# Attention probabilities transposed by DMA for six of eight head pairs, and seven half products in place of eight for gate and up of two of six feed-forward chunks

## The chip, the core and the metric

The kernel runs on one core of a Trainium2 chip. Five engines work side by side: TensorE (PE in the profile; its weight loads are PEld), VectorE (DVE), ScalarE (ACT), GpSimd (POOL) and SyncE (SP), which here only issues DMAs. The metric is the time of one execution on the device in microseconds; lower is better.

## The reference

Two layers of a streaming encoder on x of 256 tokens by 1024, all in float32. Cut to what matters:

```python
def swiglu_ffn(h, w_up, w_down):                   # w_up: 1024 x 5632, w_down: 2816 x 1024
    gate, up = jnp.split(h @ w_up, 2, axis=-1)
    return (jax.nn.silu(gate) * up) @ w_down

for l in range(2):
    x = x + 0.5 * swiglu_ffn(rms_norm(x, g_ffn1[l]), w_up1[l], w_down1[l])
    h = rms_norm(x, g_mix[l]); z = h @ w_in[l]     # LRU x and gate | q | k | v | forget logits | branch gates
    y_lru = (gelu(z_lg) * rg_lru(conv(z_lx), ...)) @ w_lru_out[l]
    # 16 heads of 64, per block of 128 queries:
    #   s = qn @ kn.T * scale + cum_q - cum_k, causal;  p = softmax(s);  o = p @ v
    y_attn = o @ w_attn_out[l]
    x = x + (gate_lru * y_lru + gate_attn * y_attn) @ w_o[l]
    x = x + 0.5 * swiglu_ffn(rms_norm(x, g_ffn2[l]), w_up2[l], w_down2[l])
```

## The kernel before

Every large product is made of three matmuls in a rounded float32 format: each operand is split into a high part and the rest, and high x high, high x low and low x high add up in one PSUM bank (`visit`, L397 to L399). Weights pass through in tiles of 256 rows by 512 columns, 128x1024 on chip, 512 KB each, numbered in one list `hcs` in the order of use. `emit_dma` (L307) loads the next tile into one of RAW = 5 buffers `raw`, on SP's queue. `emit_hi` (L331) casts it on ACT to `whi`, `emit_lo` (L340) subtracts on DVE, raw minus high, into `wlo`; RING = 6 of each exist, and a cast can go ahead once the tile six places earlier has had its last matmul. When `emit_lo` has read a raw buffer, the load of the next tile is issued into it. `block` runs a piece of 1024 x 512 weights: four tiles, first for token block 0 and then for token block 1, twelve matmuls of 512 columns a tile.

The feed-forward (`ffn`) walks over the 2816 hidden columns in six chunks `CH`, five of 512 and one of 256. For a chunk it runs gate (`ev_g`: SiLU on ACT, L637), up (`ev_u`: times the gate on DVE, L642) and then `down` of the chunk before it: for either half of the output two tiles and two token blocks. Gate and up end in PSUM banks `z`, `down` in `x` and `y`. The chunk's hidden values are turned by `h_chain`: `turn` copies them as 16-bit halves into a temporary tile (L315 on DVE or L318 on ACT, whichever the planner holds to be free first), SP issues a DMA transpose (L517), and a second copy puts the halves back; `split_seg` (L502 on ACT, L504 on DVE) makes the high and low parts.

In the mixing stage (`mix`) attention runs as chains beside the projections. `pair_chain(j)` handles two heads: eight score matmuls (L1008), a masked minimum on DVE (L1024), exponentials on ACT (L1033), scaling, six 128x128 transposes on PE (`quad`, L481), two copies out of PSUM into `pt` (L315, L318), and `pv_chain` multiplies with the values (L1070). At most NLIVE = 2 pairs are under way. After the gates and the LRU output projection the kernel needs all pairs (`S.need(att)`) before the attention output projection.

The order on every engine is fixed when the program is built. A planner (`Sched`) keeps an estimated time for each engine; after each half tile of matmuls its `hook` steps the chains that are due. The hardware then runs each engine's instructions in that order, each waiting for its semaphores. GpSimd has little work: powers for the norms (L551, L950), constants at the start, and DMAs of small rows. The large scratch tiles are NSLOT = 12 slots of 8 KB a partition, handed out by `slot` and given back by `free`.

## Time and profile before

| | us |
|---|---|
| median of three runs | 1269.91 (1269.89 to 1270.96) |
| the profiled execution | 1269.92 |
| its span, first to last instruction | 1268.2 |
| PE busy | 1257.6 (99%) |
| DVE busy | 825.4 (65%) |
| ACT busy | 804.8 (63%) |
| POOL busy | 69.5 (5%) |
| mean granted TensorE clock | 1.000 of full speed |

Feed-forwards lie at about 12 to 190, 455 to 640, 640 to 818 and 1082 to 1268 us, mixing between them. Times in rows are microseconds from the start of the span unless ns is said; a matmul's shown length includes its pipeline, so that lengths of neighbours overlap. `x3` is a count. What stands in brackets after an instruction is the idle time of its engine before it and who ended that.

### The profile page before, as it was taken

Reading aid. Unit: us, or ns where it says so; the run is one execution under the profiler, and the core shown is the slowest. Engines: PE = TensorE matmul, PEld = TensorE weight load, DVE = VectorE, ACT = ScalarE, POOL = GpSimd, SP = SyncE. Lnnn points to the kernel's source line nnn. Section 1 sums busy time; section 2 is a strip of 40 time slices with the busy share of each in tenths; the row PEclk is TensorE's granted clock in tenths of the full one; section 3 lists DMA queues with packets and bytes.
Section 4 is the critical chain, followed back from the end, with each engine's and each line's share of the span. In section 5 each row is a group of like instructions: output and inputs, shape, how many; then the busy total and the mean of one; then the engine's idle time right before and its main releaser. Section 6 shows DMA issues by size and latency. Waiting matters only on the chain.

```text
span 1268.2 us, 16349 instructions
## 1 busy us (share of the span) xinstructions
PE 1257.6 (99%) x5961; PEld 1039.6 (82%) x5961; DVE 825.4 (65%) x1164; ACT 804.8 (63%) x1076; POOL 69.5 (5%) x89
## 2 busy tenths in 40 slices
PE   9999999999999999999999999999999999999998
PEld 7888888888777888888888888888887878888887
DVE  6655558798676666555575545678977767655553
ACT  6657557886767556555566555679757764665553
POOL 4000000002200000000000000000042000000000
PEclk9999999999999999999999999999999999999999
DMA  7967769676444568676678777597764345687762
GB/s 258 264 207 225 217 172 277 161 218 202 148 141 150 168 198 217 209 208 207 179 220 217 213 216 216 158 249 190 210 206 149 126 150 182 193 222 216 216 199 76
DMA packets 193489, 248.80 MB, mean 196 GB/s; under 512 B 73672, under 2 KB 86144, under 8 KB 193408
## 3 DMA queue, kind: packets, MB, share of 16 engines
q1 hardware_dynamic: 191472, 244.49, 64.8%
q0 software_dynamic: 1920, 3.26, 1.0%
q8 instruction: 47, 0.77, 0.2%
q14 instruction: 34, 0.28, 0.1%
q10 hardware_dynamic: 16, 0.00, 0.0%
HBM read 229.88 MB, written 2.10 MB: 183 GB/s over the span
## 4 chain that ended last, share of the span: by engine, by line
PE 94%; DVE 3%; ACT 1%; DMA 1%; issue 1%; SPq 0%; POOL 0%; ACTq 0%; DVEq 0%
PE x L397 14%; PE x L399 13%; PE x L398 13%; PE z L398 12%; PE z L397 12%; PE z L399 12%; PE y L397 4%; PE y L399 4%; PE y L398 4%; PE z L481 2%; PE z L1008 1%; PE z L818 1%; DVE wlo L340 1%; PE y L1070 1%; DMA raw<-in_w_up_dram 1%
## 5 line engine op out<-in xcount | busy, mean ns | idle before, releaser
L340 DVE TENSOR_TENSOR wlo<-raw,whi 128x1024 fp32r<-128x1024 f32 x423 | 510.3, 1221 | 218.8 <-ACT whi L331 211.4
L331 ACT CAST whi<-raw 128x1024 fp32r<-128x1024 f32 x423 | 440.3, 1049 | 209.2 <-PE z L399 118.0
L397 PE MATMUL x<-whi,s 128*128 128x512 f32 x800 | 322.4, 403 | 4.8 <-DVE nat L954 2.8
L399 PE MATMUL x<-whi,s 128*128 128x512 f32 x800 | 312.5, 391 | 0.0
L398 PE MATMUL x<-wlo,s 128*128 128x512 f32 x800 | 312.2, 390 | 0.0
L398 PE MATMUL z<-wlo,s 128*128 128x512 f32 (+1 forms) x752 | 279.5, 372 | 0.1
L397 PE MATMUL z<-whi,s 128*128 128x512 f32 (+1 forms) x752 | 279.3, 371 | 0.0
L399 PE MATMUL z<-whi,s 128*128 128x512 f32 (+1 forms) x752 | 279.1, 371 | 0.0
L397 PEld LDWEIGHTS x<-whi,s 128*128 128x128 f32 x800 | 150.3, 188 | 38.8 <-issue 2.9
L399 PEld LDWEIGHTS x<-whi,s 128*128 128x128 f32 x800 | 150.2, 188 | 33.3 <-DVE s L504 0.9
L398 PEld LDWEIGHTS x<-wlo,s 128*128 128x128 f32 x800 | 150.5, 188 | 29.4 <-DVE wlo L340 0.6
L398 PEld LDWEIGHTS z<-wlo,s 128*128 128x128 f32 x752 | 141.7, 188 | 25.9 <-DVE wlo L340 1.8
L397 PEld LDWEIGHTS z<-whi,s 128*128 128x128 f32 x752 | 141.7, 188 | 24.4
L399 PEld LDWEIGHTS z<-whi,s 128*128 128x128 f32 x752 | 141.7, 188 | 24.4
L318 ACT COPY tmp<-nat 128x1024 uint16<-128x1024 uint16 (+1 forms) x88 | 96.3, 1114 | 76.2 <-DMA nat<-tmp 68.2
L397 PE MATMUL y<-whi,s 128*128 128x512 f32 x208 | 82.3, 396 | 0.0
L399 PE MATMUL y<-whi,s 128*128 128x512 f32 x208 | 81.1, 390 | 0.0
L398 PE MATMUL y<-wlo,s 128*128 128x512 f32 x208 | 81.0, 390 | 0.0
L642 DVE SCALAR_TENSOR_TENSOR nat<-z,rstd,nat 128x512 f32<-128x512 f32 (+1 forms) x48 | 33.9, 706 | 57.9 <-PE z L399 57.9
L504 DVE TENSOR_TENSOR s<-tmp,s 128x512 fp32r<-128x512 f32 (+1 forms) x71 | 46.6, 657 | 27.4 <-ACT s L502 26.9
L637 ACT ACTIVATE nat<-z,rstd 128x512 f32<-128x512 f32 (+1 forms) x46 | 30.0, 652 | 47.1 <-PE z L399 47.0
L502 ACT CAST s<-tmp 128x512 fp32r<-128x512 f32 (+1 forms) x71 | 42.0, 592 | 20.6 <-DVE tmp L531 19.8
(161 smaller groups left out, 891.0 us busy)
## 6 DMA issues: line engine op xcount, KB each, us to landing
raw<-in_w_up_dram SPq DMA_DIRECT2D x175, 512.0 KB, 4.6
raw<-in_w_in_dram SPq DMA_DIRECT2D x112, 512.0 KB, 4.4
raw<-in_w_down_dram SPq DMA_DIRECT2D x88, 512.0 KB, 4.4
raw<-in_w_lru_out_dram SPq DMA_DIRECT2D x16, 512.0 KB, 3.8
raw<-in_w_attn_out_dram SPq DMA_DIRECT2D x16, 512.0 KB, 3.8
raw<-in_w_o_dram SPq DMA_DIRECT2D x16, 512.0 KB, 4.3
s<-ones_d POOLq DMA_DIRECT2D x16, 128.0 KB, 4.4
tmp<-in_b_gate_dram SPq DMA_DIRECT2D x8, 256.0 KB, 4.3
```

What stands on the lines that cost most here:

```text
L318: nc.scalar.copy(out_, in_)
L331: nc.scalar.copy(hi, raws[i])
L340: nc.vector.tensor_tensor(out=lo, in0=raws.pop(i), in1=f32(hi), op=ALU.subtract)
L397: nc.tensor.matmul(acc, lhsT=lhs(0, k0 + kk)[:, ts], rhs=hi[:, kk, :], start=st, stop=False)
L398: nc.tensor.matmul(acc, lhsT=lhs(0, k0 + kk)[:, ts], rhs=lo[:, kk, :], start=False, stop=False)
L399: nc.tensor.matmul(acc, lhsT=lhs(1, k0 + kk)[:, ts], rhs=hi[:, kk, :], start=False, stop=sp)
L481: nc.tensor.transpose(dst_ps[:, j * P:(j + 1) * P], src[:, j * P:(j + 1) * P], ident)
L502: nc.scalar.copy(hi, t)
L504: nc.vector.tensor_tensor(out=lo, in0=t, in1=f32(hi), op=ALU.subtract)
L637: nc.scalar.activation(s[tok][0], acc, AF.Silu, scale=rs(tok))
L642: nc.vector.scalar_tensor_tensor(out=h, in0=acc, scalar=rs(tok), in1=h, op0=ALU.mult, op1=ALU.mult)
L818: nc.tensor.matmul(ps[:, g, :], lhsT=wax[0][:, g, n, :], rhs=xr[0][:, n, :], start=True, stop=True)
```

## The change

Gate and up of chunks 2 and 4 (`SEVEN`) are one product of a 2 x 2 block matrix (token block by half of k) with another (half of k by gate or up). In place of eight block products seven are made, of sums of blocks (Winograd's form): 84 matmuls of 512 columns instead of 96. The four weight blocks "11", "12", "22", "21" (half of k; gate, up) are loaded by eight DMAs straight into five slots, all at the moment when the load ahead of them is issued. GpSimd makes four sums of weight blocks, t3 = 22 - 12, t1 = 12 - 11, t2 = t3 + 11, t4 = 21 - t2, each in two operations on 128x1024. The products run in the order 11, t1, t2, 21, t3, 22, t4, each over two tiles that are cast and subtracted as before but used for one product only. Once a feed-forward, GpSimd also makes sums of the normalised input, in six operations, which are split once. The results are put together by seven additions on DVE (each with one operand in PSUM) and one copy on ACT, then go through SiLU and product as before.

In attention, pairs 0 to 5 of eight transpose their probabilities with `turn`: a copy to 16-bit halves, a DMA transpose of 128x768 words, and a copy back, in place of six PE transposes and two copies. Four pairs may be under way instead of two; six `pair` buffers take the place of `pr` and `pt`.

To make room RAW goes from 5 to 4; the constants `ones`, `lft` and `g1row` move to pooled tiles (`lft` is now filled by two DVE memsets in every layer), the buffers of `logsig` go from two to one; and the transposes of the small parameter rows come 45 us earlier in the plan. The diff, cut to its core:

```diff
-RAW = 5
+RAW = 4
 NSLOT = 12
 NNAT = 4
 NTMP = 3
-NLIVE = 2
+NLIVE = 4
+NPAIR = 6
 LEAD = 3
 SLACK = 2.5
 IDLE = 1.6
 HSTEP = 3.0
+GPS = 2.3
...
+SEVEN = (2, 4)
...
-        hcs.append((w[r0:r0 + nk * P, c0:c0 + ncol].rearrange("(k p) n -> p k n", p=P), nk, ncol))
+        loads.append((w[r0:r0 + nk * P, c0:c0 + ncol].rearrange("(k p) n -> p k n", p=P), len(hcs)))
+        hcs.append((nk, ncol))
+        uses.append(NT)
+    ORDER = ("11", "t1", "t2", "21", "t3", "22", "t4")
+    class Seven:
+        def __init__(self):
+            self.i0 = len(hcs)
+            self.t, self.chain = {}, None
+        def index(self, name, u):
+            return self.i0 + 2 * ORDER.index(name) + u
+        def part(self, name, u):
+            return self.t[name][0][:, 2 * u:2 * u + 2]
+        def load(self, name, u, src):
+            if not self.t:
+                for k in ("11", "12", "22", "21", "t3"):
+                    self.t[k] = slot([P, 4, 512])
+            nc.sync.dma_start(out=self.part(name, u), in_=src)
+            if name != "12":
+                raws[self.index(name, u)] = self.part(name, u), 0.0
+            if (name, u) == ("21", 1):
+                self.chain = S.add(self.sums(), S.now + 6.0, "g")
+        def sums(self):
+            def op(name, u, dst, a, b, f):
+                o = self.part(dst, u)
+                nc.gpsimd.tensor_tensor(out=o, in0=self.part(a, u), in1=self.part(b, u), op=f)
+                raws[self.index(name, u)] = o, S.use("g", GPS)
+            for u in range(2):
+                op("t3", u, "t3", "22", "12", ALU.subtract)
+                yield S.t["g"], "g"
+                op("t1", u, "12", "12", "11", ALU.subtract)
+                yield S.t["g"], "g"
+            for name, dst, a, b, f in (("t2", "11", "t3", "11", ALU.add), ("t4", "21", "21", "11", ALU.subtract)):
+                for u in range(2):
+                    while nxt["lo"] <= self.index(dst, u):
+                        yield S.now + 0.5, "g"
+                    op(name, u, dst, a, b, f)
+                    yield S.t["g"], "g"
+        def release(self):
+            for t in self.t.values():
+                free(t)
+    sevens = []
+    def plan_seven(w, f0):
+        st = Seven()
+        sevens.append(st)
+        for name, r0, c0 in (("11", 0, f0), ("12", 0, FF + f0), ("22", 512, FF + f0), ("21", 512, f0)):
+            for u in range(2):
+                r = r0 + 256 * u
+                loads.append((w[r:r + 256, c0:c0 + 512].rearrange("(k p) n -> p k n", p=P), (st, name, u)))
+        for _ in range(14):
+            hcs.append((2, 512))
+            uses.append(1)
...
+            if c in SEVEN:
+                plan_seven(wu, f0)
+            else:
+                plan_block(wu, f0, n)
+                plan_block(wu, FF + f0, n)
...
-        src, nk, ncol = hcs[i]
+        src, i = loads.pop(0)
+        nk, ncol = hcs[i]
         t = new(raw_p, [P, nk, ncol], "raw")
         for c in range(cuts):
             ks = slice(c * nk // cuts, (c + 1) * nk // cuts)
             nc.sync.dma_start(out=t[:, ks], in_=src[:, ks])
-        raws[i] = t
+        raws[i] = t, 0.0
+        while loads and isinstance(loads[0][1], tuple):
+            src, (st, name, u) = loads.pop(0)
+            st.load(name, u, src)
...
-        emit_dma()
+        if uses[i] == NT:
+            emit_dma()
...
+        def sums_chain():
+            for tok in range(NT):
+                for hf in range(2):
+                    yield nrm.done[tok, hf]
+            xh, xl = nrm.xT[0][0], nrm.xT[1][0]
+            a, b = slot([P, KD, T]), slot([P, 4, 4, P])
+            for q in range(2):
+                yield S.t["g"], "g"
+                ks = slice(4 * q, 4 * q + 4)
+                nc.gpsimd.tensor_tensor(out=a[0][:, ks], in0=f32(xh[:, ks]), in1=f32(xl[:, ks]), op=ALU.add)
+                S.use("g", GPS)
+            A = lambda tok, q: a[0][:, 4 * q:4 * q + 4, tok * P:(tok + 1) * P]
+            B = lambda i: b[0][:, i]
+            for i, u, v, f in ((0, A(1, 0), A(1, 1), ALU.add), (1, B(0), A(0, 0), ALU.subtract),
+                               (2, A(0, 0), A(1, 0), ALU.subtract), (3, A(0, 1), B(1), ALU.subtract)):
+                yield S.t["g"], "g"
+                nc.gpsimd.tensor_tensor(out=B(i), in0=u, in1=v, op=f)
+                S.use("g", GPS / 2)
+            free(a)
+            sums[0], sums[1] = slot([P, 4, 4, P], F32R), slot([P, 4, 4, P], F32R)
+            yield S.t["g"], "a"
+            for q in range(2):
+                ii = slice(2 * q, 2 * q + 2)
+                yield from split_seg(b[0][:, ii], sums[0][0][:, ii], sums[1][0][:, ii], 1024)
+                yield S.now, "a"
+            free(b)
...
+        def seven(c):
+            st = sevens.pop(0)
+            S.need(sums_c)
+            xh = lambda tok, q: lambda e, k: nrm.xT[e][0][:, 4 * q + k, tok * P:(tok + 1) * P]
+            xs = lambda i: lambda e, k: sums[e][0][:, i, k, :]
+            w = slot([P, 4, 512])
+            s1, u2, u4, c22 = (w[0][:, i] for i in range(4))
+            h, b5 = {}, []
+            def prod(name, lhs_, fin):
+                b, r = zbank()
+                for u in range(2):
+                    visit(st.index(name, u), b, lhs_, 2 * u, None, u == 0, u == 1, (lambda: fin(b, r)) if u else None)
...
+            def after_1(b, r):
+                nc.scalar.copy(s1, b)
+                S.use("a", act_c(512))
+                r.free = True
+            def after_6(b, r):
+                plus(u2, b, s1)
+                r.free = True
+                plus(u4, b5[0], u2)
+            def after_2(b, r):
+                end = plus(s1, b, s1)
+                r.free = True
+                gate(0, s1, end)
+            def after_7(b, r):
+                plus(u2, b, u2)
+                r.free = True
+                plus(c22, b5[0], u2)
+                b5[1].free = True
+            def after_3(b, r):
+                end = plus(u4, b, u4)
+                r.free = True
+                up(0, u4, end)
+            def after_4(b, r):
+                end = plus(u2, b, u2)
+                r.free = True
+                up(1, c22, gate(1, u2, end))
+            prod("11", xh(0, 0), after_1)
+            prod("t1", xs(0), lambda b, r: b5.extend((b, r)))
+            prod("t2", xs(1), after_6)
+            prod("21", xh(0, 1), after_2)
+            prod("t3", xs(2), after_7)
+            prod("22", xs(3), after_3)
+            prod("t4", xh(1, 1), after_4)
...
+                assert hpos[0] == sevens[0].i0
+                seven(c)
+            else:
+                block(lhs, ev_g, xbank if c < mixed else zbank, n, nrm if c == 0 else None, c < mixed)
+                block(lhs, ev_u, zbank, n)
...
+            lft, rl = new_tmp([P, NT + 1, P])
+            nc.vector.memset(lft[:, :NT], 0.0)
+            nc.vector.memset(lft[:, NT], 1.0)
...
-            pr = new(att_p, [P, 2, 3 * P], "pr")
-            mn = new(sm_p, [P, 4], "mn")
-            sums = new(sm_p, [P, 4], "sums")
+            pr, rp = new_pair()
...
-            yield end, "p"
-            pz = []
-            for e in range(2):
-                pz.append(zbank())
-                quad(pr[:, e], pz[e][0], 3)
-            if j >= 2:
-                yield pv_c[j - 2]
-            pt = new(att_p, [P, 2, 3 * P], "pt")
-            end = 0.0
-            for e in range(2):
-                yield S.now, "a"
-                end = max(end, copy_any(pt[:, e], pz[e][0][:, :3 * P], 3 * P, S.now))
-                pz[e][1].free = True
-            pv_c[j] = S.add(pv_chain(j, pt), end, "p", True, LATE)
-        def pv_chain(j, pt):
+            if j < H // 2 - 2:
+                yield end, "a"
+                pt, rt = new_pair()
+                b6 = lambda t: t.rearrange("p e (m t) -> p (e m) t", t=P)
+                yield from turn(pr.rearrange("p e n -> p (e n)"), rp, b6(pt), b6(pt), end)
+                end = S.cur.ready
+            else:
+                yield end, "p"
+                pz = []
+                for e in range(2):
+                    pz.append(zbank())
+                    quad(pr[:, e], pz[e][0], 3)
+                rp.free = True
+                pt, rt = new_pair()
+                for e in range(2):
+                    yield S.now, "a"
+                    end = max(end, copy_any(pt[:, e], pz[e][0][:, :3 * P], 3 * P, S.now))
+                    pz[e][1].free = True
+            pv_c[j] = rt.user = S.add(pv_chain(j, pt, rt), end, "p", True, LATE)
+        def new_pair():
+            r = S.claim(att_ring, NPAIR)
+            return new(att_p, [P, 2, 3 * P], "pair"), r
+        def pv_chain(j, pt, rt):
...
-                live.append(S.add(pair_chain(j), S.now, "p", True, LATE))
+                pairs.append(S.add(pair_chain(j), S.now, "p", True, LATE))
+                live.append(pairs[j])
...
-        yield S.now + 70.0, "p"
+        yield S.now + 25.0, "p"
...
```

## Rows read from the trace of the kernel before

**Rows 1.** The page: busy time of engines, and shares of the ending chain.
```profile
PE 1257.6 (99%) x5961; PEld 1039.6 (82%) x5961; DVE 825.4 (65%) x1164; ACT 804.8 (63%) x1076; POOL 69.5 (5%) x89
...
PE 94%; DVE 3%; ACT 1%; DMA 1%; issue 1%; SPq 0%; POOL 0%; ACTq 0%; DVEq 0%
```

**Rows 2.** Busy time by stretch: a `down` piece, then gate and up of chunk 2.
```profile
core 0: us, PE busy (x) PEld busy (x) DVE busy (x) ACT busy (x) POOL busy (x), PEclk, DMA share, GB/s
...
500.00:511.00 11.00, 11.00 (x50) 9.12 (x49) 5.98 (x6) 6.76 (x8) 0.00 (x0) 1.00 0.95 268
511.00:533.00 22.00, 22.00 (x98) 18.21 (x97) 11.77 (x12) 11.46 (x14) 0.00 (x0) 1.00 0.56 179
```

**Rows 3.** Timeline of PE: start, length; first matmuls of chunk 2 and behind it.
```profile
511.03 0.39 PE L397 MATMUL z<-whi,s 128*128 128x512 f32 x1
...
532.79 0.39 PE L397 MATMUL x<-whi,s 128*128 128x512 f32 x1
```

**Rows 4.** Instructions by line and shape: count | busy us, mean ns | idle before.
```profile
L340 DVE TENSOR_TENSOR wlo<-raw,whi 128x1024 fp32r<-128x1024 f32 x423 | 510.3, 1221 | 218.8 <-ACT whi L331 211.4
L331 ACT CAST whi<-raw 128x1024 fp32r<-128x1024 f32 x423 | 440.3, 1049 | 209.2 <-PE z L399 118.0 <-PE x L399 53.7 <-ACT tmp L318 12.9
...
L318 ACT COPY tmp<-nat 128x1024 uint16<-128x1024 uint16 x72 | 85.2, 1207 | 56.5 <-DMA nat<-tmp 56.5
...
L504 DVE TENSOR_TENSOR s<-tmp,s 128x512 fp32r<-128x512 f32 x63 | 43.2, 686 | 20.1 <-ACT s L502 19.7
...
L315 DVE COPY tmp<-nat 128x1024 uint16<-128x1024 uint16 x24 | 16.7, 698 | 3.6 <-DMA nat<-tmp 3.0
...
L318 ACT COPY pt<-z 128x384 f32<-128x384 f32 x20 | 8.8, 480 | 11.7 <-PE z L481 11.6
```

**Rows 5.** Timeline of POOL at the start: start, length.
```profile
0.80 0.20 POOL masks.py:197 MEMSET ident<- 128x128 f32 x1 [0.29 <-POOLq L1285]
1.08 0.29 POOL masks.py:199 TENSOR_SCALAR_AFFINE_SELECT ident<-ident 128x128 f32<-128x128 f32 x1
...
1.83 0.31 POOL L1190 MEMSET posm<- 128x256 f32 x1
```

**Rows 6.** Timeline of POOL: four power operations.
```profile
189.73 0.56 POOL L551 TENSOR_TENSOR rstd<-msum,mhalf 128x1 f32<-128x1 f32 x1 [80.72 <-DVE msum L549]
...
298.81 1.67 POOL L950 TENSOR_TENSOR rq<-rq,mhalf 128x8 f32<-128x8 f32 x1 [57.72 <-DVE rq L948]
...
311.91 2.57 POOL L950 TENSOR_TENSOR rq<-rq,mhalf 128x8 f32<-128x8 f32 x1 [3.46 <-DVE rq L948]
...
461.43 0.87 POOL L551 TENSOR_TENSOR rstd<-msum,mhalf 128x1 f32<-128x1 f32 x1 [5.80 <-DVE msum L549]
```

**Rows 7.** Timeline of DVE beside those four.
```profile
189.47 0.68 DVE L588 SCALAR_TENSOR_TENSOR xn<-y,xn 128x512 f32<-128x512 f32 x1
...
299.60 1.22 DVE L340 TENSOR_TENSOR wlo<-raw,whi 128x1024 fp32r<-128x1024 f32 x1 [0.87 <-ACT whi L331]
...
311.73 3.69 DVE L340 TENSOR_TENSOR wlo<-raw,whi 128x1024 fp32r<-128x1024 f32 x3
...
461.20 0.68 DVE L504 TENSOR_TENSOR s<-tmp,s 128x512 fp32r<-128x512 f32 x1
```

**Rows 8.** Timeline of DVE ahead of chunk 2 of the second feed-forward.
```profile
486.47 2.59 DVE L340 TENSOR_TENSOR wlo<-raw,whi 128x1024 fp32r<-128x1024 f32 x2 [0.52 <-ACT whi L331]
...
501.02 2.35 DVE L340 TENSOR_TENSOR wlo<-raw,whi 128x1024 fp32r<-128x1024 f32 x2
```

**Rows 9.** The page, DMA issues: count, size, median us to landing.
```profile
raw<-in_w_up_dram SPq DMA_DIRECT2D x175, 512.0 KB, 4.6
...
nat<-tmp SPq DMA_TRANSPOSE x64, 4.6
```

**Rows 10.** Line L340 alone: count, ns min/median/max, first and last start.
```profile
L340 DVE TENSOR_TENSOR wlo<-raw,whi x423: 1198/1224/1228, 10.0 to 1249.3; 128x1024 fp32r<-128x1024 f32 x141
```

**Rows 11.** Busy time by stretch, as in rows 2: the attention pairs of layer 0.
```profile
330.00:395.00 65.00, 63.91 (x350) 50.57 (x349) 46.91 (x129) 49.59 (x116) 6.65 (x3) 1.00 0.40 131
```

**Rows 12.** The ending chain in order of time: start, us, what; one pair's transposes.
```profile
366.19 0.65 PE z L481 x6
```

## The prediction: what the rows say the change will do

> **What bounds the kernel now.** I read the page first: TensorE (PE) is busy for 99% of the span, and 94% of the chain that ended last is PE [rows 1]. Then the timeline of PE inside one gate-and-up chunk: first matmul of the chunk at 511.03 us, first matmul of the next piece at 532.79, so 96 matmuls in 21.76 us, 0.2267 us from start to start with no gap [rows 3]. The 0.39 us that a single one shows is its pipelined length, not its price. The granted clock is 1.00 throughout, so a matmul taken away is worth 0.2267 us as long as the rest keeps up. The rest is VectorE (DVE) and ScalarE (ACT), which split every weight tile (ACT casts `whi`, DVE subtracts to get `wlo`): in that chunk DVE works 11.77 of 22 us, ACT 11.46, and GpSimd (POOL) not at all [rows 2]. So there is room, but it has to be filled exactly where the change needs it.
>
> **What leaves PE.** A chunk of gate and up has 2 token blocks x 2 outputs x 8 k x 3 terms = 96 matmuls. Seven products of 4 k x 3 terms are 84. Twelve fewer, times 0.2267, is 2.72 us a chunk; two chunks in each of four feed-forwards make eight, so 21.8 us. The six transposes of a pair take 0.65 us on PE [rows 12]; six pairs in two layers are 12 x 0.65 = 7.8 us. Together 29.6 us is the most the change can give: 1269.9 - 29.6 = 1240.
>
> **What comes on DVE and ACT for one such chunk.** The seven products use 14 tiles of 128x1024, each for one product, where the ordinary chunk uses 8 tiles for two tokens each. So 14 casts and 14 subtractions instead of 8: six more of 1.05 us on ACT and six more of 1.22 us on DVE (1.13 back to back: two ended 2.35 us after the first began) [rows 4, 8]. Seven additions from PSUM on DVE, at the 0.69 us of a 128x512 operation [rows 4], are 4.8 us, and one 128x512 copy on ACT. PE needs a new tile every 6 x 0.2267 = 1.36 us; alone, DVE at 1.13 plus 0.34 for the additions' share is a little over that, and ACT at 1.05 is under it. The six ring buffers can carry it over such a deficit, if they are full at the start.
>
> **The window that decides.** I lay the new chunk where chunk 2 of the second feed-forward lies now. The eight direct loads are issued together, behind the last load of the `down` piece before them, which waits for a raw buffer: with four raw buffers that is the subtraction that ended at 486.47 + 2.59 = 489.06 [rows 8]. A 512 KB load lands 4.4 to 4.6 us after issue [rows 9], and at the 268 GB/s of the busy `down` stretch [rows 2] each further one takes 1.96 us. The fifth of the eight (block "22", first half), which the first POOL operation needs, is the sixth in line: 489.1 + 4.5 + 5 x 1.96 = 503.4. PE wants the last of the 14 tiles at 511.03 + 13 x 1.36 = 528.7. So 25.3 us, in which all eight POOL operations and twelve of the 14 subtractions (two, on block "11", need no sum and now stand at 501.02) must be through.
> - DVE in it: 12 x 1.13 + two `L504` splits of the previous chunk and the gate-times-up, 3 x 0.69, = 15.7 us with both inputs in SBUF; six additions with a PSUM input, 4.1 us. Sum 19.8 of 25.3: it fits alone.
> - ACT: 12 x 1.05, two SiLU, one copy, two casts, at most two copies of 1.2: about 18 of 25.3. It fits.
> - POOL: no row shows a POOL operation on two tiles of 1024 elements a partition. The nearest: a memset of 128 elements 0.20 us, of 256 elements 0.31, so 0.86 ns an element and 0.09 fixed; an affine select, which also reads, 0.29 at 128 elements, so a read adds 0.70 ns an element [rows 5]. Two reads and a write: 0.09 + 1.024 x (0.86 + 1.40) = 2.4 us. Bounds: four memsets of 256, 1.24 us, and three times that, 3.7. I take 2.4: 19.2 us for eight. It fits alone.
>
> **DVE against POOL.** Now the rows that make me doubt it. POOL's power operation on 128x8 took 1.67 us at 298.81, and 2.57 at 311.91, where a DVE subtraction of two SBUF tiles had begun 0.18 us earlier and had about 1.05 to go. On 128x1 it took 0.87 us beside the two-input `L504` (461.20), but 0.56 beside `L588` (189.47), one of whose inputs is PSUM [rows 6, 7]. So a POOL operation that reads SBUF waits for the end of a DVE operation with two SBUF inputs, and not for one with a PSUM input. The other direction is not shown: POOL's reads here are of 8 elements and over at once (the subtraction at 299.60 began inside a POOL operation and took its normal 1.22 [rows 6, 7]). If POOL's reads hold DVE in the same way, the times add: 15.7 + 19.2 = 34.9 us into 25.3, 9.6 us late. If only the read part holds (2 x 0.70 x 1.024 = 1.43 us an operation, 11.4 in all): 15.7 + 11.4 = 27.1, 1.8 us late. I take 6 us, near the middle.
> The Trainium skill (SBUF — State Buffer, section "Who interferes with whom") states this as a rule: a DVE operation with two SBUF inputs and a GpSimd operation that reads SBUF exclude each other, and whichever comes second waits for the whole of the first. The trace agrees with it for POOL coming second (2.57 against 1.67 us) and shows nothing for DVE coming second. By the rule the whole-operation end, 9.6 us late, would hold. A price of its own has GPSIMD Engine Reference, section "Performance versus the Vector engine" of the Trainium skill: 4497 ns for 2048 elements, so an estimate of 2.25 us here, by which the chunk would be 8.4 us late; no run here shows it.
>
> **The other parts.** Each feed-forward also makes sums of the normalised input: six POOL operations (two of full size, four of half: 9.6 us), two casts, two subtractions, in chunks 0 and 1, whose pieces load DVE much as those of [rows 2] do; taken at 1 us a feed-forward, bounds 0 and 3, 4 us in all. A pair's two copies of 128x1536 uint16 cost at most 1.5 x 1.21 on ACT or 1.5 x 0.70 on DVE each, in place of two of 0.48 [rows 4]: 2.7 us more on ACT or about 1.1 on DVE a pair. Between 330 and 395 us ACT works 49.6 of 65 and DVE 46.9 [rows 11]; six pairs shared between them fit. The transpose's landing (4.6 us [rows 9]) lengthens a pair, but four live pairs take the place of two. I give 1 us back a layer, bounds 0 and 4: -7.8 + 2 = -6. The transposes of h, issued on SP behind the eight loads, land up to 8 us later; the ACT copy that waits for them holds the casts behind it, but `down` needs them only after the chunk: 0 now, up to 2 us a chunk if casts of the sums stand behind it. At nothing: one raw buffer fewer (four loads ahead at 2.72 us of PE each still exceed 4.6 us of landing; without that cover a load's rest, 1 to 2 us a tile), the constants moved to pooled tiles, the earlier row transposes, memsets moved to DVE (under 1 us a layer, beside matmuls).
>
> **The sum.** Forecast: 8 x (6.0 - 2.72) = +26, sums +4, attention -6: +24 us. The profiled execution took 1269.92 us, its span 1268.2 and 1.7 around it, and the median is 1269.91, so no correction: **1294 us**. With the two ends of the lock, 1.8 and 9.6 us late: 8 x (-0.9) - 6 + 4 = -9, 1261; and 8 x 6.9 + 4 - 6 = +53, 1323.
>
> **Rivals.**
> - *POOL does not hold DVE (faster).* Then only POOL's own row counts: six operations (sums t3, t1, t2) from 503.4 at 2.4 us end at 517.8, cast and subtraction make it 520, and PE wants that tile at 511.03 + 5 x 1.36 = 517.8: some 1 to 2 us late a chunk, less if loads land faster. 8 x (1.2 - 2.72) - 6 = -18: **1252**, from 1242 (never late, 1 us kept on the rest) to 1260. For it: no subtraction of the 423 was ever stretched (1198 to 1228 ns is their whole spread [rows 10]). Against it: none ever came second to a long POOL read. It decides as soon as a subtraction that starts inside a POOL operation ends in 1.22 us.
> - *The two cancel.* Lock on the reads only, or POOL earlier than I place it: late by 2 to 3.5 us a chunk, 1262 to 1276, middle **1269**.
> - That the 84 matmuls don't appear can't be: the counts are fixed in the code.
>
> **How the numbers follow.** Forecast case (1276 to 1323) 0.50; POOL harmless (1242 to 1262) 0.40; cancelling 0.10. A measurement here tells 0.2%, about 2.5 us. Of the cancelling case 0.06 lie within that, 0.03 below, 0.01 above: faster 0.43, same 0.06, slower 0.51. Cases of both signs hold the chance; the likeliest one's own range is 1276 to 1316. The range for 8 in 10 leaves out about a tenth on each side: 1246 to 1316.
>
> **What the profile after would show.** Right: `wlo` subtractions of 2 to 3.5 us in chunks 2 and 4, beside POOL operations; POOL operations over 3 us; PE waiting for `wlo` there by 4 us or more a chunk; the other chunks as before. The rival: subtractions still at 1.22, POOL at about 2.4 throughout, a chunk of gate and up within 20 to 21 us. The attention step is right if the transposes of `pr` fall from 96 to 24 and the stretch between its ends is some 3 us a layer shorter. I am wrong on the loads if the first POOL operation of a chunk starts far from 7 to 8 us ahead of the chunk's first matmul (503.4 against 511.0), and wrong altogether if the gap comes from SP's queue or from DMA waits of ACT.

## The result, and the profile after

The changed kernel takes **1380.38 us** (1378.45 to 1384.25) against 1269.91 before: ratio 1.0868, 95% interval 1.0855 to 1.0880. Slower was the forecast, but at 1294 us, with a range that ended at 1316: the forecast was 86 us short.

The page of the changed kernel, to be held against [rows 1]: busy time, the granted TensorE clock in 40 slices, and the ending chain.

```profile
PE 1268.7 (92%) x5793; PEld 1021.6 (74%) x5793; DVE 1013.1 (74%) x1266; ACT 880.7 (64%) x1154; POOL 308.5 (22%) x176
...
PEclk9879999999999999999999999999999999999999
...
PE 58%; DVE 17%; DMA 11%; issue 7%; ACT 4%; POOL 2%; SPq 0%; DVEq 0%; ACTq 0%; POOLq 0%
DVE wlo L414 12%; PE x L478 11%; PE x L479 10%; PE x L480 10%; DMA nat<-tmp 6%; PE z L479 5%; PE z L478 5%; PE z L480 5%; DVE s L582 2%; DMA raw<-in_w_up_dram 2%; PE y L478 2%; PE y L480 2%; PE y L479 2%; DMA raw<-in_w_down_dram 2%; DVE s L755 1%
```

TensorE has 168 matmuls and transposes fewer (96 and 72, as counted), and yet is busy 11 us longer; the chain has left it for DVE and DMA. The instructions by line and shape (count, busy us, mean ns, idle before), to be held against [rows 4]; `L414` is the old `L340`, `L582` the old `L504`, `L280` the sums of weights on POOL, `L755` the seven additions:

```profile
L414 DVE TENSOR_TENSOR wlo<-raw,whi 128x1024 fp32r<-128x1024 f32 x359 | 453.3, 1286 | 92.8 <-ACT whi L405 89.6 <-PE z L480 0.3
...
L414 DVE TENSOR_TENSOR wlo<-s,whi 128x1024 fp32r<-128x1024 f32 x112 | 185.6, 1697 | 64.2 <-ACT whi L405 64.2
L280 POOL TENSOR_TENSOR s<-s,s 128x1024 f32<-128x1024 f32 x64 | 183.9, 2894 | 341.0 <-DMA s<-in_w_up_dram 292.7 <-DVE wlo L414 47.0
...
L582 DVE TENSOR_TENSOR s<-tmp,s 128x512 fp32r<-128x512 f32 x63 | 60.1, 955 | 33.2 <-ACT s L580 32.9
L755 DVE TENSOR_TENSOR s<-z,s 128x512 f32<-128x512 f32 x56 | 38.3, 684 | 0.6
```

Subtractions for the seven products take 1697 ns in the mean in place of 1221 (half of them at most 1216, the longest 3443), splits 955 in place of 686; the additions, one of whose inputs is PSUM, are not stretched (684).

Where the time went is read by stage. Each stage ends with the second of two `rstd` operations on POOL (before: 200.70, 461.43, 645.64, 827.90, 1088.57 us), here three of the changed kernel in the timeline of POOL:

```profile
249.78 0.86 POOL L629 TENSOR_TENSOR rstd<-msum,mhalf 128x1 f32<-128x1 f32 x1 [12.79 <-DVE msum L627]
...
505.77 0.87 POOL L629 TENSOR_TENSOR rstd<-msum,mhalf 128x1 f32<-128x1 f32 x1 [5.79 <-DVE msum L627]
...
716.62 0.56 POOL L629 TENSOR_TENSOR rstd<-msum,mhalf 128x1 f32<-128x1 f32 x1 [12.53 <-DVE msum L627]
```

Differences of such starts, for this kernel and for runs told below (us; ff is a feed-forward, the last one to the end of the span):

| | ff 1 | mixing | ff 2 | ff 3 | mixing | ff 4 |
|---|---|---|---|---|---|---|
| before | 200.7 | 260.7 | 184.2 | 182.3 | 260.7 | 179.6 |
| after | 249.8 | 256.0 | 210.9 | 204.3 | 256.2 | 199.6 |
| attention part alone (e1) | 203.7 | 259.2 | 187.4 | 184.2 | 256.1 | 179.8 |
| POOL additions in the kernel before (e6) | 210.1 | 261.3 | 195.2 | 194.4 | 260.7 | 190.4 |
| no weight sums (e2) | 231.8 | 255.8 | 191.9 | 194.1 | 256.0 | 184.9 |
| the same, rows early, loads spread (e9) | 218.9 | 255.9 | 188.8 | 188.7 | 256.3 | 177.4 |
| no sums, no additions (e14) | 209.2 | 256.4 | 180.7 | 178.9 | 255.8 | 174.1 |

The mixing stages gain 4.5 us each; the feed-forwards lose 49, 27, 22 and 20.

How such a loss comes about shows in chunk 2 of the second feed-forward, where the prediction laid its window. The timeline of SP's queue, ACT, POOL, DVE and PE there, line by line in that order of engines:

```profile
535.14 6.43 SPq L271 DMA_DIRECT2D s<-in_w_up_dram  x8
...
544.51 5.57 SPq L595 DMA_TRANSPOSE nat<-tmp  x1
...
554.57 1.36 ACT L392 COPY tmp<-nat 128x1024 uint16<-128x1024 uint16 x1 [7.88 <-DMA nat<-tmp]
...
547.21 16.16 POOL L280 TENSOR_TENSOR s<-s,s 128x1024 f32<-128x1024 f32 x6 [26.90 <-DMA s<-in_w_up_dram]
...
556.86 1.50 DVE L414 TENSOR_TENSOR wlo<-s,whi 128x1024 fp32r<-128x1024 f32 x1 [9.15 <-ACT whi L405]
558.29 2.88 DVE L582 TENSOR_TENSOR s<-tmp,s 128x512 fp32r<-128x512 f32 x1
561.09 4.50 DVE L414 TENSOR_TENSOR wlo<-s,whi 128x1024 fp32r<-128x1024 f32 x2
...
559.71 0.39 PE L478 MATMUL z<-whi,s 128*128 128x512 f32 x1
564.51 0.51 PE L479 MATMUL z<-wlo,s 128*128 128x512 f32 x1 [4.42 <-DVE wlo L414]
...
566.37 0.63 PE L478 MATMUL z<-whi,s 128*128 128x512 f32 x1
566.80 0.63 PE L479 MATMUL z<-wlo,s 128*128 128x512 f32 x1
```

The transpose of h, issued behind the eight direct loads, lands at 554.54, 10 us after its issue; ACT waits 7.88 us with the copy of it, the casts stand behind that copy, and DVE has nothing to subtract for 9.15 us. POOL meanwhile adds, mostly alone. When the casts come, POOL is still at it: a split of 0.69 us takes 2.88, two subtractions 4.50, and PE stops for 4.42 us. The stretches (us, busy us of PE, PEld, DVE, ACT, POOL, then the granted clock, DMA share, GB/s):

```profile
550.00:555.00 5.00, 5.00 (x24) 4.14 (x23) 0.00 (x0) 0.43 (x1) 4.87 (x3) 1.00 1.12 346
...
560.00:565.00 5.00, 0.58 (x3) 0.44 (x3) 5.00 (x3) 3.16 (x4) 3.37 (x2) 1.00 0.00 0
565.00:570.00 5.00, 5.00 (x17) 3.92 (x16) 5.00 (x6) 4.78 (x6) 1.40 (x1) 0.66 0.02 3
```

DVE works 0 of 5 us in the first stretch, and 5 of 5 in the other two; behind PE's gap of 4.42 us the granted clock is 0.66, and matmuls start 0.43 us apart instead of 0.227 (the levels of 1.2 and 2.4 GHz). On the page, a transpose of h lands 5.9 us after issue in the median, 4.6 before [rows 9], and a direct load after 9.2:

```profile
s<-in_w_up_dram SPq DMA_DIRECT2D x64, 512.0 KB, 9.2
...
nat<-tmp SPq DMA_TRANSPOSE x64, 5.9
```

### The profile page after: what moved, and what is told of

It reads as the page before. It is cut to its first block, busy times and chain, and to the rows that moved or that the text cites. A ratio compares the mean times of both kernels' runs of the same rounds, so it can differ in the third digit from the quotient of the medians.

```text
span 1376.7 us, 16385 instructions
## 1 busy us (share of the span) xinstructions
PE 1268.7 (92%) x5793; PEld 1021.6 (74%) x5793; DVE 1013.1 (74%) x1266; ACT 880.7 (64%) x1154; POOL 308.5 (22%) x176
## 4 chain that ended last, share of the span: by engine, by line
PE 58%; DVE 17%; DMA 11%; issue 7%; ACT 4%; POOL 2%; SPq 0%; DVEq 0%; ACTq 0%; POOLq 0%
DVE wlo L414 12%; PE x L478 11%; PE x L479 10%; PE x L480 10%; DMA nat<-tmp 6%; PE z L479 5%; PE z L478 5%; PE z L480 5%; DVE s L582 2%; DMA raw<-in_w_up_dram 2%; PE y L478 2%; PE y L480 2%; PE y L479 2%; DMA raw<-in_w_down_dram 2%; DVE s L755 1%
## 5 line engine op out<-in xcount | busy, mean ns | idle before, releaser
L414 DVE TENSOR_TENSOR wlo<-raw,whi 128x1024 fp32r<-128x1024 f32 x359 | 453.3, 1286 | 92.8 <-ACT whi L405 89.6
L405 ACT CAST whi<-raw 128x1024 fp32r<-128x1024 f32 x359 | 368.3, 1047 | 165.1 <-PE x L480 44.9
L479 PE MATMUL x<-wlo,s 128*128 128x512 f32 x800 | 316.1, 395 | 13.7 <-DVE wlo L414 13.7
L478 PE MATMUL z<-whi,s 128*128 128x512 f32 (+1 forms) x720 | 273.4, 380 | 10.3 <-ACT whi L405 9.5
L480 PE MATMUL z<-whi,s 128*128 128x512 f32 (+1 forms) x720 | 272.1, 378 | 0.0
L280 POOL TENSOR_TENSOR s<-s,s 128x1024 f32<-128x1024 f32 x64 | 183.9, 2894 | 341.0 <-DMA s<-in_w_up_dram 292.7
L414 DVE TENSOR_TENSOR wlo<-s,whi 128x1024 fp32r<-128x1024 f32 x112 | 185.6, 1697 | 64.2 <-ACT whi L405 64.2
L392 ACT COPY tmp<-nat 128x1024 uint16<-128x1024 uint16 (+1 forms) x92 | 100.6, 1095 | 81.9 <-DMA nat<-tmp 79.7
L405 ACT CAST whi<-s 128x1024 fp32r<-128x1024 f32 x112 | 114.2, 1047 | 34.4 <-POOL s L280 24.4
L629 POOL TENSOR_TENSOR rstd<-msum,mhalf 128x1 f32<-128x1 f32 x12 | 8.2, 684 | 414.2 <-DVE msum L627 414.2
L582 DVE TENSOR_TENSOR s<-tmp,s 128x512 fp32r<-128x512 f32 (+1 forms) x71 | 63.5, 895 | 47.4 <-ACT s L580 47.0
L1145 POOL TENSOR_TENSOR rq<-rq,mhalf 128x8 f32<-128x8 f32 x16 | 34.9, 2182 | 249.7 <-DVE rq L1143 236.4
L478 PE MATMUL y<-whi,s 128*128 128x512 f32 x208 | 82.7, 397 | 0.0
```

The costliest lines, as they stand in the source:

```text
L280: nc.gpsimd.tensor_tensor(out=o, in0=self.part(a, u), in1=self.part(b, u), op=f)
L392: nc.scalar.copy(out_, in_)
L405: nc.scalar.copy(hi, raws[i][0])
L414: nc.vector.tensor_tensor(out=lo, in0=raws.pop(i)[0], in1=f32(hi), op=ALU.subtract)
L478: nc.tensor.matmul(acc, lhsT=lhs(0, k0 + kk)[:, ts], rhs=hi[:, kk, :], start=st, stop=False)
L479: nc.tensor.matmul(acc, lhsT=lhs(0, k0 + kk)[:, ts], rhs=lo[:, kk, :], start=False, stop=False)
```

## The experiments

Theory: the sums of weights on POOL hold DVE (the lock), and that is the loss. Rivals: the loads and transposes on SP's queue; POOL's own queue; DVE's additional work. Each ratio is against the kernel before on the same chip (1270.3 to 1270.7 us).

**e1: the attention part alone.**
```
-SEVEN = (2, 4)
+SEVEN = ()
```


> The changed kernel with the attention part alone: all six feed-forward chunks are multiplied as before, no sums on POOL; four raw buffers, the earlier row transposes and the moved constants stay. Theory (the attention step was right, all of the loss comes from the seven products): between the ends of the two mixing stages the changed kernel is 4.7 and 4.4 us shorter than before, so 1269.9 - 9.1 = 1261 us, and no feed-forward longer by more than 1 us. Rival (the fourth raw buffer or the earlier row transposes cost something of their own): the first feed-forward stays longer, 1270 us or more.


1269.66 us, 0.9994 [0.9984, 1.0003]. The mixing stages gain 1.5 and 4.6, but the first three feed-forwards, in which nothing of the attention happens, lose 2 to 3 each, which is the sign of the rival: something else of the change costs there (e5).

**e2: no sums of weights.** The products take blocks that aren't summed; 64 POOL operations are left out.
```
-  nc.gpsimd.tensor_tensor(out=o, in0=self.part(a, u), in1=self.part(b, u), op=f)
-  raws[self.index(name, u)] = o, S.use("g", GPS)
+  raws[self.index(name, u)] = self.part("11" if a == "t3" else a, u), S.use("g", GPS)
```


> The changed kernel without the eight GpSimd operations a chunk that make the sums of weight blocks (64 in all): the products take an unsummed block in their place, so that part of the computation is left out; matmuls, casts, subtractions, loads and the sums of the input stay. Theory (POOL's reads hold the subtractions, and this is most of what a chunk loses): feed-forwards 2 to 4 fall from 210.9, 204.3 and 199.6 us to within 6 us of 184, 182 and 180, the whole to 1380 - 64 = 1316 us or less, and every subtraction is back at 1.22 us. Rival (the transposes of h that wait behind the eight direct loads, with ACT standing still behind them, are most of it): no more than 2 us a chunk comes back, 1364 us or more.


1312.79 us, 1.0328 [1.0301, 1.0355]. The sums cost 67.6 us, 8.4 a chunk, and the subtractions for the seven products are back at 1218 ns; 42 us above the kernel before remain, and feed-forwards 2 and 3 stay 8 and 12 us above it, where the theory allowed 6. So the sums are the largest part and not the whole. Nor are the 67.6 us all lock: with the sums also go casts that waited for the sums themselves (24.4 us on ACT in the changed kernel) and part of a wait in the first feed-forward that e4 shows.

**e3: the direct loads issued on ACT's queue.** `nc.sync` becomes `nc.scalar` in `load`.


> The changed kernel with the eight direct loads of a chunk issued from ACT's queue instead of SP's, nothing else. Theory of the queue: a transpose of h no longer stands behind 4 MB of loads, lands within 5 to 6 us of its issue instead of 10, and ACT's idle time ahead of its second copy falls from 66 to under 40 us; 3 to 4 us a chunk come back, 1348 to 1356 us. Theory of the lock: what sets the chunk is POOL and DVE in turn, and only what ACT lost ahead of the chunk comes back, under 1.5 us a chunk: 1368 us or more.


1401.03 us, 1.1015 [1.0986, 1.1044]; slower still. The timeline of ACT and its queue:

```profile
534.74 9.48 ACTq L271 DMA_DIRECT2D s<-in_w_up_dram  x5
544.26 1.05 ACT L405 CAST whi<-raw 128x1024 fp32r<-128x1024 f32 x1 [8.85 <-DMA s<-in_w_up_dram]
```

Issuing five loads held ACT for 9.48 us, and the casts with it. The transposes did land sooner, as the theory of the queue had it (4.8 us in the median for 5.9; ACT's waits for them fell from 79.7 to 21.0 us in the span), and yet the whole got longer: the burst does harm on whichever of the two queues it stands.

**e4: the 24 row loads issued at the start.** `yield 20.0` becomes `yield 0.0` in `rows_chain`.


> The changed kernel with the 24 small row loads put on POOL's queue 20 us earlier in the plan, so that they stand ahead of the sums of the input and not among them; the row transposes and the copies of ones come 20 us earlier with them. Theory (POOL's order is what the first feed-forward loses beyond the others, 49 against 20 to 27 us): ACT no longer waits 15.4 us for the last sum, 15 to 25 us come back, 1355 to 1365 us. Rival (the first feed-forward is slow from its fuller DMA queues and from one raw buffer less): under 5 us, 1375 us or more.


1363.6 us, 1.0744 [1.0710, 1.0778]: 16.8 us back. What stood there, in the changed kernel's timeline of POOL and ACT, and its stretches:

```profile
31.05 0.74 POOL L545 DMA_DIRECT2D s<-in_g_ffn_dram  x1
...
44.87 0.58 POOL L550 DMA_DIRECT2D bfb<-in_b_forget_dram  x1
45.48 1.27 POOL L726 TENSOR_TENSOR s<-s,s 128x512 f32<-128x512 f32 x1
...
46.78 1.04 ACT L580 CAST s<-s 128x1024 fp32r<-128x1024 f32 x1 [15.35 <-POOL s L726]
```

```profile
40.00:50.00 10.00, 0.80 (x1) 0.29 (x1) 1.19 (x2) 3.21 (x4) 6.73 (x12) 0.64 0.06 6
50.00:60.00 10.00, 9.91 (x37) 7.59 (x38) 8.95 (x10) 6.73 (x8) 0.00 (x0) 0.85 0.86 202
```

The last sum of the input stood behind 24 DMA issues of about 0.5 us on POOL; ACT waited 15.35 us with the cast of it, with all casts behind, and PE worked 0.80 of 10 us. Before the change POOL had nothing in that place that anybody waited for.

A second wait lies in the same stage. `ones_chain` makes two tiles of ones on ACT (copies of `ident`), and POOL issues the DMAs that store each; it comes behind the row transposes, so the change put it earlier too. POOL and its queue in the changed kernel, and ACT's wait (us in all, times, the longest):

```profile
72.70 9.56 POOL L280 TENSOR_TENSOR s<-s,s 128x1024 f32<-128x1024 f32 x4 [25.95 <-DMA s<-in_w_up_dram]
82.21 1.31 POOL L872 DMA_DIRECT2D ones_d<-s  x2
...
ACT s L868 <- DMA ones_d<-s: 14.9, 1, 14.9
```

ACT waits 14.9 us, to 86.42, to write the second tile until the first is stored, and that store is issued only at 82.21, behind four weight sums on POOL; PE waits 5.30 us for the cast behind it (at 92.48). In the kernel before, ACT copies five of the eight quarters from 102.88 to 108.17 without a wait. The second tile waits for the first because it gets the same slot: by the kernel's list of free slots a single one of the twelve is left there, as chunk 2 already holds its five. The wait (4.4 to 9.9 us elsewhere) stands in e2, e3, e9, e11, e13, e14 and e15, whose lists hold one slot there too, and in none of e1, e4, e7, e17 and e18, whose lists hold six or more. Of these e1, e4, e7 and e17 have the earlier place as well, so the place alone doesn't make it. The 16.8 us of e4 thus hold two waits, the one behind the DMA issues and this one.

**e5: the kernel before with four raw buffers.** `RAW = 5` becomes `RAW = 4`.


> The kernel before with four raw buffers in place of five, nothing else. With the attention part alone the second rstd of a feed-forward's end comes 12.5 to 13.7 us after the first, where the kernel before takes 11.0, at three places. Theory A: that is the price of the fifth raw buffer, so some 2.2 us at each of three boundaries: 1276 us (1273 to 1279). Rival B: it comes from the DMA transposes or the earlier row loads, and four buffers cost nothing, as the prediction had it: 1270 (1268.5 to 1271.5).


1276.25 us, 1.0044 [1.0029, 1.0059]. The fifth buffer is worth 5.6 us; against e5, the attention part of e1 gives 1276.25 - 1269.66 = 6.6 us.

**e6: the lock by itself, in the kernel before.** Ahead of gate and up of chunks 2 and 4 in the order of the program, on a spare buffer that nobody reads:
```
+  nc.gpsimd.memset(junk[0], 1.0)
+  for _ in range(8):
+      nc.gpsimd.tensor_tensor(out=junk[0][:, 2:], in0=junk[0][:, :2], in1=junk[0][:, 2:], op=ALU.add)
```


> The kernel before, with one memset and eight POOL additions of 128x1024 on a spare buffer, read by nobody, ahead of gate and up of chunks 2 and 4 of every feed-forward; so the hold between POOL and DVE alone, without sums that anybody waits for. Theory A (they exclude each other for a whole operation): subtractions beside them 1.7 us and more in place of 1.22, POOL additions 2.6 to 2.9; DVE works 11.8 of the 22 us of such a chunk, so 19.2 us of POOL make 31 of 22: up to 9 us late a place, less what the ring gives, 8 places: 1290 to 1340. Theory B (only the read part holds): 11.8 + 11.4 = 23.2 of 22: 1270 to 1283. Rival C (POOL does not hold DVE): subtractions at 1.22, 1269 to 1271.


1314.04 us, 1.0343 [1.0326, 1.0361]: 43.4 us, 5.4 for each of the eight groups of additions. Nothing holds POOL back until the chunk, so that in the second to fourth feed-forward both groups run one behind the other from the stage's start, most of it ahead of chunk 2: this is the price of the lock by itself, but not at the place where the changed kernel has it. The timeline of POOL and DVE in the second feed-forward:

```profile
474.09 25.19 POOL L650 TENSOR_TENSOR s<-s 128x1024 f32<-128x1024 f32 x8
...
501.11 24.46 POOL L650 TENSOR_TENSOR s<-s 128x1024 f32<-128x1024 f32 x8
...
504.24 10.11 DVE L340 TENSOR_TENSOR wlo<-raw,whi 128x1024 fp32r<-128x1024 f32 x3
514.27 2.90 DVE L504 TENSOR_TENSOR s<-tmp,s 128x512 fp32r<-128x512 f32 x1
...
520.45 0.74 DVE L642 SCALAR_TENSOR_TENSOR nat<-z,rstd,nat 128x512 f32<-128x512 f32 x1
521.22 2.11 DVE L315 COPY tmp<-nat 128x1024 uint16<-128x1024 uint16 x1
```

Three subtractions in 10.11 us, 3.37 each; a split 2.90; an operation with a PSUM input its normal 0.74. A DVE operation on two SBUF tiles and a POOL addition follow one another in turn: 1.13 back to back [rows 8] and about 2.2 us of POOL make the 3.37. That DVE waits for the whole POOL operation is what the Trainium skill says (SBUF — State Buffer, section "Who interferes with whom"), and here the trace agrees. The uint16 copy, 0.70 us otherwise [rows 4] and with a single input, is held too, 2.11.

**e7, e9: no weight sums, rows early; and the direct loads spread.** e7 is e2 and e4 together. e9 reorders the loads:
```
+  loads[i - 3:i + 8] = [raw_[0], *own[:2], raw_[1], *own[2:4], raw_[2], *own[4:]]
```


> The changed kernel without the 64 weight sums on POOL (the products take the unsummed blocks, so that part of the computation is left out), and with the 24 row loads issued at the start. Without the weight sums alone it took 1312.8, and its first feed-forward was still 31 us longer than before. Theory A: that part is POOL's queue, the sums of the input behind the row loads, and goes with the earlier loads: 1312.8 - 17 (what the earlier loads gave with the sums) = 1296, down to 1285 if all of the excess in that feed-forward goes. Rival B: the excess there is from the eight direct loads, as in the other feed-forwards, and stays: 1307 to 1313.

> As the run without weight sums and with early row loads (1305.0 us), and the eight direct loads of a chunk no longer issued together: two behind each of the last three loads of the down piece before, the last four behind the third. The weight sums are left out as there. Theory A (the transposes of h stand behind the burst on SP's queue; ACT waited 22.7 us and DVE 14.0 us for them in the first feed-forward, ACT 24 in the second): at most two to four loads stand ahead of a transpose, so half or more of that goes: 1272 to 1292. Rival B (the 14 subtractions and seven additions keep DVE busy 9 of 10 us there, and that alone makes PE wait): 1301 to 1308.


e7 1304.97 us, 1.0267 [1.0250, 1.0285], between its two expectations; e9 1288.09, 1.0152 [1.0131, 1.0174], as its theory A had it. Early rows give 7.8 us without the sums (16.8 with them), and spreading the loads 16.9, 2.1 a chunk; ACT's waits for the transposes of h fall from 88.3 to 66.1 us in the span. The 16.9 us are net of a loss: the loads now take the chunk's slots earlier, so the wait for the tiles of ones, gone in e7, is back in e9's first feed-forward (6.35 us on ACT, 8.96 on PE).

**e10: all DMA transposes on ACT's queue (no weight sums, rows early).** `nc.sync.dma_start_transpose` becomes `nc.scalar`.


> As the run without weight sums and with early row loads (1305.0 us), and all DMA transposes issued on ACT's queue instead of SP's; the loads stay as they are, eight together on SP. The weight sums are left out as there. Theory A (it is the order on one queue): a transpose no longer stands behind eight loads, only shares the engines with them, and lands in 4 to 6 us: 1278 to 1295, with ACT's cost of issuing against it. Theory A2 (the 16 DMA engines are full and a transpose gets its share late on any queue): 1300 to 1306. Rival B (DVE): 1303 to 1310.


1333.75 us, 1.0481 [1.0438, 1.0524], against 1305 on SP: outside all that was expected. By stage, the feed-forwards are 1.2 to 3.3 us shorter than in e7, but each mixing stage 15 longer; an issue keeps ACT's queue 1.25 us, and what else made the 15 was not followed. ACT's waits for the transposes of h fall from 88.3 to 55.1 us. In the four feed-forwards together a queue of its own gives the transposes 8.6 us, where taking the burst apart gives 13.8 by the same stages.

**e11, e15: the whole change with early rows and spread loads; and its weight sums on DVE.** In e15 `nc.gpsimd.tensor_tensor` becomes `nc.vector.tensor_tensor`; nothing is left out in either.


> The whole changed kernel, with early row loads (1363.6 us) and the direct loads spread as in the run without sums. Theory A (queue and lock are separate costs that add): it gains what that one gains over 1305.0: 1330 to 1350. Rival B (the lock alone sets the end of a chunk, so that an earlier landing only makes POOL start earlier): 1358 to 1366. Theory C (POOL starts earlier, beside the chunk before, and the ring takes part of the lock): 1315 to 1330.

> The whole changed kernel with early row loads and spread direct loads (1369.0 us), the 64 weight sums on DVE in place of POOL; nothing left out. A sum then takes DVE 1.2 us. Theory A (exclusion: a sum on POOL keeps DVE for its 2.4 to 2.9 us, or waits as long): 64 x 1.2 to 1.7 us less, 1260 to 1292 at most, 1300 to 1330 with what the order of the work gives back. Rival B (POOL's sums ran mostly beside other work of DVE, and DVE has no room for eight more operations): 1360 to 1400.


e11 1369.01 us, 1.0778 [1.0760, 1.0796], above all three expectations: spreading, which gave 16.9 without the sums, gives nothing with them. That it costs is not shown, as the interval overlaps that of e4 (1.0710 to 1.0778). e15 1325.47, 1.0424 [1.0401, 1.0448], as its theory A had it. By line and shape (`L426` is `L414` here), first e4, then e11, then e15:

```profile
L414 DVE TENSOR_TENSOR wlo<-s,whi 128x1024 fp32r<-128x1024 f32 x112 | 188.0, 1717 | 66.9 <-ACT whi L405 66.9
```

```profile
L426 DVE TENSOR_TENSOR wlo<-s,whi 128x1024 fp32r<-128x1024 f32 x112 | 226.9, 2062 | 16.9 <-ACT whi L417 16.8
L280 POOL TENSOR_TENSOR s<-s,s 128x1024 f32<-128x1024 f32 x64 | 204.0, 3207 | 301.0 <-DMA s<-in_w_up_dram 218.8 <-PE z L492 44.0 <-DVE wlo L426 37.0
```

```profile
L426 DVE TENSOR_TENSOR wlo<-s,whi 128x1024 fp32r<-128x1024 f32 x112 | 133.3, 1218 | 3.7 <-ACT whi L417 3.7
...
L280 DVE TENSOR_TENSOR s<-s,s 128x1024 f32<-128x1024 f32 x64 | 77.7, 1224 | 22.0 <-DMA s<-in_w_up_dram 20.4
```

With the loads in one burst, DVE is idle while POOL adds; with the loads spread, its idle time ahead of these subtractions falls from 66.9 to 16.9 us, and the subtractions, 1.72 us before, become 2.06, 38.9 us more in all. So the lock takes back most of it. The rest goes in the first feed-forward, which gets 5.6 us longer: there the wait for the tiles of ones is back, and PE waits 9.12 us behind it (at 61.99); the other three get 0.7, 2.0 and 0.0 shorter. The subtractions are stretched by 112 x (2.06 - 1.22) = 94 us in e11; the sums themselves take DVE 78 in e15. Here a sum on POOL takes more of DVE than the same sum on DVE.

**e13, e14: POOL out altogether; and no additions.** e13 is e9 without the sums of the input (the products take a block of it that isn't summed); e14 also leaves out the seven additions a chunk, gate and up taking a product as it is.
```
-  nc.gpsimd.tensor_tensor(out=a[0][:, ks], in0=f32(xh[:, ks]), in1=f32(xl[:, ks]), op=ALU.add)
...
-  plus(u2, b, s1)
-  plus(u4, b5[0], u2)
...
```


> The kernel without weight sums, row loads early, direct loads spread (1288.1 us), and the sums of the normalised input on POOL left out too (the products take a block of the input that isn't summed); POOL does none of the seven products' work. Theory A (the input sums are on the path: the first feed-forward is still 18 us longer than before, and PE waits for the splits of those sums): 1262 to 1275. Rival B (they are hidden, as the prediction had it with 1 us a feed-forward): 1283 to 1289.

> As e13, and the seven additions a chunk from PSUM on DVE left out (gate and up take a product as it is). Theory A (DVE is past its room in these chunks, 9 to 10 of 10 us busy, so that the 4.8 us of additions a chunk count): 8 to 30 us below e13. Rival B (they lie beside waits for loads and transposes): within 4 us of e13. All eight chunks at the full gain of their matmuls would give 1270.3 + 5.6 - 6.6 - 21.8 = 1247.5.


e13 1278.94 us, 1.0060 [1.0045, 1.0075], between its two expectations; e14 1257.80, 0.9900 [0.9883, 0.9916], 21.1 below, as its theory A had it. So the input's sums cost 9.2 (2.3 a feed-forward), and the additions 21.1, 2.6 a chunk of the 4.8 that they last. What waits for the additions is SiLU on ACT, here in the changed kernel (28.7 us in e13); and PE's weight loads wait less for the high parts that ACT makes of `down`'s and other inputs (`split_seg`) in e14, the last row, than in e13, the row above it (us in all, times, the longest):

```profile
L762 ACT ACTIVATE nat<-s,rstd 128x512 f32<-128x512 f32 x16 | 11.5, 722 | 56.1 <-DVE s L755 56.1
...
PEld x L489 <- ACT s L591: 11.5, 7, 2.9
...
PEld x L489 <- ACT s L591: 4.0, 5, 1.4
```

Between the profiled runs of e13 and e14 lie 19.1 us, of which 10.1 are idle time of PE and 9.0 matmuls that ran longer. Full gain would be 1270.3 + 5.6 - 6.6 - 21.8 = 1247.5. By stage, e5's feed-forwards less 5.4 us of matmuls make 198.4, 181.1, 178.1 and 173.8 us, and e14 has 209.2, 180.7, 178.9 and 174.1: the matmuls' gain is there in the last three, and the 10 us above 1247.5 lie in the first. The timeline of ACT and PE in e14 shows them:

```profile
49.74 4.21 ACT L870 COPY s<-ident 32x1024 f32<-32x1024 f32 x4 [5.46 <-DMA ones_d<-s]
...
55.79 0.79 PE L489 MATMUL z<-whi,s 128*128 128x512 f32 x1 [8.07 <-ACT whi L416]
```

This is the second tile of ones again, which waits for the store of the first in the one slot that is left; the casts stand behind it, PE waits 8.07 us, and behind the gap the granted clock is 0.50 from 55 to 60 us.

**e8, e12, e16, e17, e18: the attention part alone, other versions.** e8: `RAW = 5`, `NLIVE = 3`, `NPAIR = 5`. e12: that with four pairs by DMA. e16: e8 with the forget gate's second step planned 4 us later. e17: `RAW = 5`, four live pairs, six pair tiles, room from a slot shared by the mask and the running sum. e18: e17 with the row transposes at their old place.


> The attention part alone, no chunk with seven products, with five raw buffers again; room for them comes from three live pairs in place of four and five pair tiles in place of six. With four raw buffers it took 1269.7. Theory A: the two mixing stages keep 1.5 to 4.7 us each and the three feed-forward boundaries get back their 2.2: 1262 to 1266. Rival B: three live pairs don't cover the landing of a pair's transpose, the stages lose their gain: 1268 to 1272.

> The attention part alone with five raw buffers and three live pairs, and four of the eight pairs transposed by DMA instead of six. With six it took 1270.6 us, from 1265.1 at a mean clock of 1.000 to 1274.0 at 0.997. Theory A: fewer copies on ACT between 320 and 395 us leave no gap in which the clock falls, and four pairs give 2 x 4 x 0.65 = 5.2 us: 1264 to 1267. Rival B: the gaps come from the planner's order elsewhere (845 us, the forget gate's transposes), and stay: 1268 to 1273.

> The attention part alone (six pairs by DMA, five raw buffers, three live pairs: 1270.6 us, clock 0.997 to 1.000), with the second step of the forget gate planned 4 us later, so that TensorE doesn't wait for the small copy behind a transpose's copy at 847 us. Theory A (that wait of 2.1 us, and the clock that falls to half for some us behind it, are what takes the attention's gain): 1263 to 1266, clock 0.999 or 1.000. Rival B (the wait turns up at the next place): 1268 to 1272.

> The attention part alone with six pairs by DMA, six pair tiles, four live pairs and five raw buffers; the mask and the running sum of the forget gate share a spare slot, which makes the room. Theory A (what took the gain with four raw buffers was the missing buffer, +5.6 us): 1269.7 - 5.6 = 1264, from 1262 to 1266. Rival B (gaps of 1 to 2 us where the order of the work shifts, and the clock behind them, take it as with three live pairs): 1268 to 1271.

> As e17, and the row transposes at their old place, 70 us behind their loads instead of 25. Theory A (the earlier transposes cost an idle TensorE of 1.8 us at 60 to 65 us): 1 to 2 us below e17. Rival B (nothing, or the gap goes elsewhere): within 0.8 us of e17.


e8 1270.57, 0.9996 [0.9982, 1.0010]; e12 1268.58, 0.9984 [0.9975, 0.9994]; e16 1270.74, 0.9998 [0.9988, 1.0008]; e17 1267.02, 0.9973 [0.9963, 0.9983]; e18 1267.56, 0.9970 [0.9960, 0.9980]. None came to the range of its theory A; e17 and e18 beat the kernel before by 3.6 and 3.1 us, of the 7.8 that the transposes took; e12 by 1.7 of 5.2. What takes the rest moves about. Stretches of e8, and one of e16:

```profile
845.00:850.00 5.00, 3.36 (x15) 2.47 (x14) 4.75 (x11) 3.55 (x6) 0.00 (x0) 0.88 0.61 168
850.00:855.00 5.00, 5.00 (x19) 4.12 (x18) 2.25 (x5) 3.79 (x8) 0.00 (x0) 0.78 0.36 105
```

```profile
265.00:270.00 5.00, 3.96 (x12) 3.19 (x13) 4.89 (x6) 2.25 (x4) 0.00 (x0) 0.73 0.59 180
```

In e8 PE waited 1.64 us for a small copy of the forget gate on ACT (at 847.35), and the clock fell; in e16 that wait is gone and another of 1.88 us, for `wlo`, stands at 266.04. Executions of e8 lie between 1265.1 (clock 1.000) and 1274.0 (0.997). The row transposes' place makes no difference here (0.5 us between e17 and e18, with intervals of 1.3 to either side).

## Why the prediction was wrong

Undone one after another, from the changed kernel down, the terms of the sum measured as follows. Each depends on what was undone before it, and by the intervals of the two runs that it is a difference of, each is known to some 2 to 4 us:

| term | predicted, us | measured, us |
|---|---|---|
| weight sums, with their lock and what waits for them (e2) | 8 x 6.0 = 48 | 67.6 |
| row loads and POOL's queue (e7) | 0 | 7.8 (16.8 taken first, e4) |
| eight loads ahead of the transposes (e9) | 0 | 16.9 |
| sums of the input (e13) | 4 | 9.2 |
| seven additions (e14) | 0, "it fits alone" | 21.1 |
| rest, the second tile of ones in ff 1 (1257.8 less 1247.5) | 0 | 10.3 |
| one raw buffer fewer (e5) | 0 | 5.6 |
| attention (e1 against e5) | -6 | -6.6 |
| matmuls saved | -21.8 | -21.8 (taken; borne out by three of e14's stages) |

- **The matmuls** were counted right, and attention was right in size: 24 transposes of its tile in place of 96, and mixing stages 4.7 and 4.4 us shorter. Alone it keeps less of that: 1.5 and 4.6 in e1, 3.6 in all in e17.
- **The lock** was the right mechanism. Its signs are there: subtractions of 2 us and more beside POOL, PE waiting 4.42 us for `wlo`; POOL's sums are 2.89 us in the mean, short of the 3 that was named, and 3.21 in e11. By itself it costs 5.4 us a group of eight (e6, at another place), where 6 was taken between 1.8 and 9.6. The whole-operation end holds: 3.37 us a subtraction, where the read part alone would make 1.22 + 1.43 = 2.65. The rivals, POOL harmless and the lock on reads only, are out. POOL's price of 2.4 us held: four sums from 72.70 us, with DVE idle for all but the end, took 9.56. So did the window's place: the first sum at 547.21, 8.2 us ahead of the chunk's first matmul at 555.38, where 7.6 was worked out.
- **The step that failed** is the one headed "The window that decides": "Sum 19.8 of 25.3: it fits alone". It set busy time against a window as if each engine could work whenever it liked. The additions, which it had inside, cost 2.6 us a chunk, though DVE had time for them: in e13 SiLU on ACT waits 28.7 us for them, with ACT's next casts and the turning of h behind it, and PE's weight loads wait 11.5 us for ACT's splits with the additions and 4.0 without. The steps between were not followed chunk by chunk. And where ACT waits 7.88 us for a DMA, DVE loses 9.15 us of the 25.3. The prediction called itself "wrong altogether if the gap comes from SP's queue or from DMA waits of ACT"; in part it does: such waits stand beside the lock.
- **The transposes of h**, "0 now, up to 2 us a chunk if casts of the sums stand behind it": they do stand behind it, and 2.1 us a chunk is what spreading the loads gives without the weight sums. The bound was right, the value taken at the wrong end. But it is no separate cost in the changed kernel: while DVE waited, POOL had the sums to itself, and with the wait gone the lock takes most of it back (e11). Costs that hide one another can't be added up.
- **"At nothing"** failed for the raw buffer (5.6 us) and for the earlier row transposes, whose chain of ones now finds a single free slot (8 us of idle PE in e14); slots were not counted in the prediction. The cover named for the buffer, four loads ahead at 2.72 us each, is that of the steady state; it is lost where a feed-forward ends: the two `rstd` there lie 13.0 to 13.7 us apart in e5, 11.0 to 11.1 with five buffers. Why just there was not followed further.
- **POOL's queue** was asked for and not read to its end: the sums of the input were priced at their length, 9.6 us a feed-forward, hidden at 1; what was ahead of them on POOL, 24 DMA issues, was on the trace of before and not in the sum.
- **The range** ended at 1316 as its upper end held one unknown, the lock, at its worst, and everything else at nothing. The terms that the table has beside the weight sums and the two gains are 70.9 us; all together make 67.6 + 70.9 - 6.6 - 21.8 = 110.1, of 110.5 measured. That they close is no proof, as the rest is what the others leave.
- The clock belongs in the sum, too: with the same 5793 matmuls PE is busy 1268.7 us after and 1233.1 in e14. The 35.6 between are matmuls that ran longer, as those of 0.63 us at 566 did behind the gap, where the granted clock was 0.66. It is no term beside the others, but the part of each that a gap costs over its length.

## What to carry to other kernels

To see if work fits beside an engine's other work, follow what each instruction stands behind, on every queue that the change touches, and which buffers are free when it comes; busy time against a window is only a necessary condition. Before a sum of two SBUF tiles goes to POOL, look at what DVE does there: here, where DVE's operations read two SBUF tiles, the 64 sums were 43 us dearer on POOL than on DVE. And give each edit "at nothing" a price if its cover goes; here they made 62 us, nearly as much as the mechanism that was analysed.

## What the runs showed that was not expected

- POOL and DVE alternate, one operation each, for as long as both have work: three subtractions took 10.11 us, while POOL's eight took 24.46, 3.06 each, where it takes 2.39 alone. A DVE copy of uint16, with one SBUF input, is held in the same way (2.11 us against 0.70).
- A DMA issue can hold its engine: five direct loads took ACT's queue 9.48 us, a transpose behind eight loads SP's 5.57, where the one at 528.88 took 1.26.
- In e8 a stretch with PE busy 3.36 of 5 us, 1.64 of it one gap, had a granted clock of 0.88, and the next one 0.78; two stretches of e1 with 3.17 and 3.48 of 5, and those behind them, stayed at 1.00. What makes the difference was not found.
